# Two blocks of a transformer on one core: the two heads of an attention pair take turns in the value products

## Chip, cores and metric

The kernel runs on one core of a Trainium2 chip. The metric is the device time of one execution in microseconds (us), a median of several runs. TensorE (PE) multiplies matrices and loads weights (PEld), VectorE (DVE), ScalarE (ACT) and GpSimd (POOL) work on elements, SyncE (SP) and GpSimd issue transfers.

## What is computed

1024 tokens of width 1024 go through two blocks. The first has attention with 8 dilated and 8 neighbourhood heads of width 64, an output projection and a mixture of 16 experts; the second has a linear attention, two recurrences and a convolved feed-forward. The change lies in the first block's attention:

```python
# dilated: three windows per head, merged by their softmax denominators
s = einsum('bhrnqd,bhrnkd->bhrnqk', qb, kb) * HEAD_DIM ** -0.5 - slopes * dist
p = exp(where(valid, s, NEG_INF) - mx); o = einsum(p, vb) / den
out = sum(softmax(lses, axis=0)[..., None] * outs)
# neighbourhood: windows of 8 x 16 on a grid of 16 x 64 tokens, learned relative bias
s = where(mask, einsum('bhijqcd,bhijkld->bhijqckl', qb, kg) * HEAD_DIM ** -0.5 + bias, NEG_INF)
o = einsum('bhijqckl,bhijkld->bhijqcd', softmax(s, axis=(-2, -1)), vg)
```

## The kernel before

Products that need precision are split in high and low parts and made of three products each (`mm3`, L260 to L262); these are the projections. Attention goes over eight pairs of heads, four dilated (`attn_dil`), then four neighbourhood ones (`attn_na`). `proj_qk` of pair p+1 stands behind pair p in the program and reads two units of weights: 2 x 2 x 8 x 3 = 96 records on PE, each of 512 columns. In the third neighbourhood pair the last projection and the opening of the output projection come in between its halves (`mid`).

A dilated pair has two halves u, and in each the heads e = 0, 1 one after the other. For a head: eight score blocks j of 128 x 256 (L495, L496) into PSUM; VectorE adds the bias and takes the extremum (L498); ScalarE makes exponentials and their sums (L500). The statistics of two windows are brought to a common row order with two small products (`swap`, L442), merged by small VectorE steps (L506 to L516) and give factors, by which VectorE scales the eight blocks (L520). Then, for jj = 0 to 3, PE transposes four squares of 128 x 128 (L525) into one PSUM tile `tp`, ScalarE copies it to `pt` (L528; for jj = 3 VectorE, L530), and PE multiplies 128 x 64 columns of values with each square (L540) into `y`: head 0 into partitions 0 to 63, head 1 into 64 to 127. Values and weights are in f32, and the trace shows two records for each such product. `finish_pair` copies `y` (L429) and stores it.

A neighbourhood pair has two halves i; for each head and each of four column groups c: two score products of 384 columns (L578), bias and extremum (L582) against `nbias`, which GpSimd makes from the mask (L563), exponentials (L584), reciprocal (L585) and scaling (L586), three transposes (L590), a copy (L592 on ScalarE for even c, L594 on VectorE for odd), three value products (L597).

The framework's scheduler fixes the order on each engine when the program is built, by program order as priority and by its own estimate of what is ready, and it puts the waits. A tag's `bufs` is the number of buffers that its tiles share: the weights of a head (`P`) have two, the transposed ones (`PT`) three, `tp` two in PSUM, `sp` two.

Later in the kernel, the S5 recurrence has products of the same shape as the value products (L1464), from 64 columns of weights, whose outputs go by turns to partitions 0 to 63 and 64 to 127:

```python
for g in range(2):
    r = slice(64 * g, 64 * g + 64)
    nc.tensor.matmul(pz[r, i, pi % 2], E[pi // 4][:, pi % 4, i, r], U[:, 2 * pi + g], start=True, stop=True,
```

Of the kernel before, what the change touches and what calls it, by code (L numbers as in the profile page):

```python
# [12 lines left out]
OP = mybir.AluOpType  # L13
# [5 lines left out]
# Places of the experts by falling load: place 0 has room for 256 tokens, the next NMORE places for 192, the others for 128.  # L19
# JOBS: the order of work.  # L20
# [7 lines left out]
# ---------------------------------------------------------------- host layout  # L28
def _units_f(w, cols):
    """[1024, *] -> one unit [128, 8*128] per block of 128 columns (contraction on partitions)."""  # L30
    return np.stack([np.ascontiguousarray(w[:, c:c + 128]).reshape(8, 128, 128).transpose(1, 0, 2).reshape(128, 1024)
                     for c in cols])


def _units_n(w, n0, n1):
    """[K, *] -> units [128, 2*512] of two contraction tiles by 512 columns."""
    k = w.shape[0] // 256
    return np.ascontiguousarray(w[:, n0:n1]).reshape(k, 2, 128, 512).transpose(0, 2, 1, 3).reshape(k, 128, 1024)
# [24 lines left out]
def _na_mask():  # L63
# [12 lines left out]
    return out.reshape(128, 6, 384)  # L76
# [20 lines left out]
def _route_consts():  # L97
    """upper[t', t] = t' < t, what a logit's lead over another must exceed (the first wins a tie), 0..15"""
# [14 lines left out]
def prep(inp):  # L113
# [31 lines left out]
    # ---- block 2  # L145
# [40 lines left out]
# ---------------------------------------------------------------- device  # L186
class K:
# [34 lines left out]
    def wraw(self, src, eng=None, after=None):  # L222
        """a unit of weights; after: what must be there before the load may take its turn"""
# [17 lines left out]
    def rstd(self, ssq, n, out):  # L241
        """out = 1/sqrt(ssq/n + eps), [128, m]"""
# [4 lines left out]
    def rstd_pow(self, ssq, n, out):  # L247
        """out = (ssq/n + eps) ** -0.5, without the square root's activation table"""
# [15 lines left out]
    def norm_rows(self, x, gb, out, st, sq=None):  # L264
        """out = x / rms(x) * g on rows; st [128, 2]; sq: room for the squares"""
# [5 lines left out]
    def rows_T(self, xn, XH, XL, i, ps):  # L271
        """rows of token tile i to columns, hi and lo"""
# [10 lines left out]
    # ------------------------------------------------ block 1, attention  # L283
    def attention(self, rs):
        """attention heads in pairs, and the output projection"""
        nc, a = self.nc, self.a
        from contextlib import ExitStack
        with ExitStack() as st, ExitStack() as sl, ExitStack() as sr:
# [44 lines left out]
            self.mask = wk.tile([128, 6, 384], F32, name="mask_n")  # L333
# [35 lines left out]
    def tm_proj(self, out, XH, XL, W, j):  # L369
        """rows of token tile j times 512 columns of weights"""  # L370
# [5 lines left out]
    def proj_qk(self, XH, XL, p):  # L376
        """-> of two heads, q's hi over lo (the odd head: lo over hi), and k's hi twice and lo twice"""
# [54 lines left out]
    def swap(self, src, n, to_a):  # L432
        """statistics of class rows (32b+i, r) to block rows (4i+r, b), or back; src [128, n, 4]"""
# [13 lines left out]
        out = wk.tile([128, n, 4], F32, tag="swo", name="swo", bufs=2)  # L447
# [3 lines left out]
    def attn_dil(self, p, q0, k0, q1, k1):  # L451
# [18 lines left out]
        for u in range(2):  # L470
            y = ps.tile([128, 512], F32, tag="y", name="y", bufs=2)
            for e in range(2):
                PP = wk.tile([128, 8, 256], F32, tag="P", name="PP", bufs=2)
                stt = wk.tile([128, 2, 2, 4], F32, tag="stat", name="stat", bufs=3)  # A/B, nm/den, j
                for j in range(8):
                    if j % 2 == 0:
                        sp = ps.tile([128, 2, 256], F32, tag="s", name="sp", bufs=2)
                    if j < 4:
                        r = j
                        lh = Q[e][:, r, 128 * u:128 * u + 128]  # L480
                        rh = [Kk[e][:, s, r, 16:272] for s in range(2)]
                        bs = bias[e][:, 256 * (3 + u):256 * (4 + u)]
                        stj = (1, j)
                    else:
                        b = 4 * u + j - 4
                        lh = (q0, q1)[e][:, 128 * b:128 * b + 128]
                        rh = []
                        for s in range(2):
# [1530 lines left out]
```

## Time and profile before

| | us |
|---|---|
| median of 3 runs (2163.27 to 2168.06) | 2163.78 |
| span of the profiled execution | 2164.2 |
| dilated pairs in it, about | 133 to 388 |
| neighbourhood pairs, about | 388 to 580 |

The profile is of one execution. Busy times are sums over an engine's instructions without counting overlaps twice; records of PE overlap since products are pipelined, so the distance from start to start tells more than the length of one. "Clock" is the share of full speed that TensorE was granted.

### The profile page before, as it was taken

The numbers are of one execution on the slowest core, as the hardware profiler recorded it, in microseconds if no ns is written. First come the engines' busy times: TensorE is split into PE (matmuls) and PEld (weight loads), VectorE is DVE, ScalarE is ACT, GpSimd is POOL, SyncE is SP. The second block draws the span as 40 slices with busy tenths as digits, with TensorE's granted clock in tenths as the row PEclk, the third lists the DMA queues.
The fourth block names the chain that finished last, engine by engine and source line by source line (L and its number), as shares of the span: only waits on it lengthen the run. The fifth ranks groups of instructions, "written<-read, shape, count | busy, mean of one in ns | idle before, by whom it ended". The sixth has DMA issues, their size and how long they took to land.

```text
span 2164.2 us, 27190 instructions
## 1 busy us (share of the span) xinstructions
PE 2032.3 (94%) x9877; PEld 1627.9 (75%) x9877; DVE 1207.6 (56%) x2613; ACT 820.4 (38%) x1502; POOL 397.5 (18%) x508
## 2 busy tenths in 40 slices
PE   8999999998898799968999979999999999999997
PEld 6878887776687577746877667778888888888886
DVE  4146666555667677758277378854443444443445
ACT  4245544444433477745321653431122111122113
POOL 2111111333342111106255143210000000000001
PEclk9999999999999799988999989999999999999999
DMA  6153322423342799957351276461111111111101
GB/s 238 69 125 92 97 77 61 106 75 105 110 129 74 255 309 316 322 191 261 115 105 44 69 257 209 147 243 40 49 49 59 49 46 37 46 58 49 49 10 78
DMA packets 123232, 260.71 MB, mean 120 GB/s; under 512 B 21872, under 2 KB 67216, under 8 KB 122448
## 3 DMA queue, kind: packets, MB, share of 16 engines
q1 hardware_dynamic: 103584, 195.94, 28.1%
q0 software_dynamic: 16800, 61.61, 8.9%
q10 hardware_dynamic: 2704, 1.31, 0.3%
q8 instruction: 81, 1.33, 0.3%
q14 instruction: 63, 0.52, 0.1%
HBM read 196.10 MB, written 53.22 MB: 115 GB/s over the span
## 4 chain that ended last, share of the span: by engine, by line
PE 43%; DVE 5%; POOL 2%; DMA 2%; issue 1%; ACT 1%; SPq 0%; POOLq 0%; DVEq 0%; ACTq 0%
PE pu L260 4%; PE pu L262 4%; PE pu L261 4%; PE pv L262 4%; PE pd L260 4%; PE pv L261 4%; PE pv L260 4%; PE pd L262 4%; PE pd L261 4%; PE pvg L262 1%; PE pvg L260 1%; PE pvg L261 1%; PE pp L260 1%; PE pp L262 1%; PE pp L261 1%
## 5 line engine op out<-in xcount | busy, mean ns | idle before, releaser
L237 ACT CAST whi<-wraw 128x1024 fp32r<-128x1024 f32 x188 | 197.4, 1050 | 608.4 <-PE pd L262 189.9
L238 DVE TENSOR_TENSOR wlo<-wraw,whi 128x1024 fp32r<-128x1024 f32 x162 | 197.9, 1222 | 271.9 <-ACT whi L237 269.0
L260 PE MATMUL pp<-XH,whi 128*128 128x512 f32 x416 | 168.2, 404 | 0.6 <-DVE kk L404 0.5
L261 PE MATMUL pp<-XL,whi 128*128 128x512 f32 x416 | 167.7, 403 | 0.0
L262 PE MATMUL pp<-XH,wlo 128*128 128x512 f32 x416 | 166.7, 401 | 0.0
L1940 DVE TENSOR_TENSOR res<-pd,res 128x512 f32<-128x512 f32 x176 | 118.4, 689 | 85.0 <-PE pd L262 85.0
L260 PE MATMUL pd<-whi,fah 128*128 128x512 f32 x352 | 138.3, 393 | 0.0
L260 PE MATMUL pu<-XH,whi 128*128 128x512 f32 x352 | 137.8, 392 | 0.0
L261 PE MATMUL pu<-XL,whi 128*128 128x512 f32 x352 | 137.6, 391 | 0.0
L262 PE MATMUL pu<-XH,wlo 128*128 128x512 f32 x352 | 137.6, 391 | 0.0
L261 PE MATMUL pd<-wlo,fah 128*128 128x512 f32 x352 | 137.1, 389 | 0.0
L262 PE MATMUL pv<-XH,wlo 128*128 128x512 f32 x352 | 137.0, 389 | 0.0
L260 PE MATMUL pv<-XH,whi 128*128 128x512 f32 x352 | 136.9, 389 | 0.0
L261 PE MATMUL pv<-XL,whi 128*128 128x512 f32 x352 | 136.9, 389 | 0.0
L1954 POOL TENSOR_TENSOR fo<-res,gfin 128x1024 f32<-128x1024 f32 x3 | 8.0, 2691 | 698.1 <-DVE res L1940 698.1
L262 PE MATMUL pd<-whi,fal 128*128 128x512 f32 x352 | 131.8, 390 | 0.0
L260 PEld LDWEIGHTS pp<-XH,whi 128*128 128x128 f32 x416 | 79.0, 190 | 18.4 <-issue 3.1
L262 PEld LDWEIGHTS pp<-XH,wlo 128*128 128x128 f32 x416 | 78.8, 189 | 15.9 <-issue 2.5
L261 PEld LDWEIGHTS pp<-XL,whi 128*128 128x128 f32 x416 | 79.0, 190 | 15.3 <-issue 2.4
L238 POOL TENSOR_TENSOR wlo<-wraw,whi 128x1024 fp32r<-128x1024 f32 x26 | 62.7, 2413 | 144.0 <-ACT whi L237 105.0
L1926 DVE TENSOR_TENSOR ft<-ft,pv 128x1024 f32<-128x1024 f32 x22 | 26.9, 1222 | 103.2 <-PE pv L262 103.2
L500 ACT ACTIVATE PP<-PP,stat 128x256 f32<-128x256 f32 x128 | 64.4, 504 | 48.0 <-DVE stat L498 44.1
(563 smaller groups left out, 4901.8 us busy)
## 6 DMA issues: line engine op xcount, KB each, us to landing
wraw<-in_wgu_dram SPq DMA_DIRECT2D x64, 512.0 KB, 4.7
wraw<-in_wup_dram SPq DMA_DIRECT2D x44, 512.0 KB, 3.3
wraw<-in_wdn_dram SPq DMA_DIRECT2D x32, 512.0 KB, 5.0
wraw<-in_wdown_dram SPq DMA_DIRECT2D x22, 512.0 KB, 3.3
O<-ot SPq DMA_DIRECT2D x17, 512.0 KB, 4.9
wraw<-in_win_f_dram SPq DMA_DIRECT2D x16, 512.0 KB, 4.2
x<-x_d SPq DMA_DIRECT2D x16, 512.0 KB, 4.1
x_d<-x SPq DMA_DIRECT2D x16, 512.0 KB, 3.7
```

The source lines that it names most:

```text
L237: nc.scalar.copy(hi, raw)
L238: (eng or nc.vector).tensor_tensor(lo, raw, hi.bitcast(F32), op=OP.subtract)
L260: nc.tensor.matmul(out, lh, rh, start=start, stop=False, **kw)
L261: nc.tensor.matmul(out, lh, rl, start=False, stop=False, **kw)
L262: nc.tensor.matmul(out, ll, rh, start=False, stop=stop, **kw)
L500: nc.scalar.activation(PP[:, j], PP[:, j], AF.Exp, bias=nm, scale=-1.0, accum_out=stt[:, stj[0], 1, stj[1]:stj[1] + 1])
L1926: V.tensor_tensor(t, t, pv, op=OP.mult)
L1940: V.tensor_tensor(self.res[:, j, cn], pd, self.res[:, j, cn], op=OP.add)
L1954: nc.gpsimd.tensor_tensor(o, x, gb, op=OP.mult)
```

## The change

In both kinds of pair the softmax of both heads now comes first, and then the transposes and value products, in which the heads take turns. In the dilated pairs the softmax of a head moves into `dil_weights`, called for both heads; for each jj both heads' squares are transposed and copied, and then the products go i by i, head 0, head 1. In the neighbourhood pairs the scores and softmax of both heads and all four c come first, then c by c both heads' transposes and copies, and their products t by t, head 0, head 1.

The weights of a head are kept in two tiles of half the size, with five such buffers for both heads; `PT` has four. Room for that comes from a mask in bf16 instead of f32 and from fewer buffers of `swo`, `stat`, `mg`, `nM`, `fac`, `statn` and `r1` (the output projection's row factor). Comments are taken out all over the file.

```diff
-    return out.reshape(128, 6, 384)
+    return out.reshape(128, 6, 384).astype(mybir.dt.np(BF16))
...
-            self.mask = wk.tile([128, 6, 384], F32, name="mask_n")
+            self.mask = wk.tile([128, 6, 384], BF16, name="mask_n")
...
-        out = wk.tile([128, n, 4], F32, tag="swo", name="swo", bufs=2)
+        out = wk.tile([128, n, 4], F32, tag="swo", name="swo", bufs=1)
...
             y = ps.tile([128, 512], F32, tag="y", name="y", bufs=2)
-            for e in range(2):
-                PP = wk.tile([128, 8, 256], F32, tag="P", name="PP", bufs=2)
-                stt = wk.tile([128, 2, 2, 4], F32, tag="stat", name="stat", bufs=3)  # A/B, nm/den, j
-                for j in range(8):
...
-                # merge the two softmaxes
...
-                for j in range(8):
-                    f = fb[:, 0, j:j + 1] if j < 4 else fac[:, 0, j - 4:j - 3]
-                    nc.vector.tensor_scalar(PP[:, j], PP[:, j], f, None, op0=OP.mult)
-                for jj in range(4):
+            both = [self.dil_weights(u, e, (q0, q1)[e], Q[e], Kk[e], bias[e]) for e in range(2)]
+            for jj in range(4):
+                pts = []
+                for e, PP in enumerate(both):
                     tp = ps.tile([128, 4, 128], F32, tag="tr", name="tp", bufs=2)
-                    pt = wk.tile([128, 4, 128], F32, tag="PT", name="PT", bufs=3)
+                    pt = wk.tile([128, 4, 128], F32, tag="PT", name="PT", bufs=4)
                     for i in range(4):
-                        nc.tensor.transpose(tp[:, i], PP[:, 2 * jj + i // 2, 128 * (i % 2):128 * (i % 2) + 128],
-                                            self.ident)
+                        nc.tensor.transpose(tp[:, i], PP[jj // 2][:, 2 * (jj % 2) + i // 2,
+                                                                  128 * (i % 2):128 * (i % 2) + 128], self.ident)
                     if jj != 3:
                         nc.scalar.copy(pt, tp)
                     else:
                         nc.vector.tensor_copy(pt, tp)
-                    for i in range(4):
-                        j, kt = 2 * jj + i // 2, i % 2
+                    pts.append(pt)
+                for i in range(4):
+                    j, kt = 2 * jj + i // 2, i % 2
+                    for e, pt in enumerate(pts):
                         if j < 4:
                             yo = y[64 * e:64 * e + 64].rearrange("p (m r) -> p r m", r=4)[:, j]
                             v = VB[:, kt, j, 64 * e:64 * e + 64]
...
                         nc.tensor.matmul(yo, v, pt[:, i], start=(j == 0 and kt == 0), stop=(j == 7 and kt == 1),
                                          skip_group_check=True)
             self.finish_pair(p, u, y)
+    def dil_weights(self, u, e, q, Qr, Kr, bias):
+        nc, wk, ps = self.nc, self.wk, self.ps
+        PP = [wk.tile([128, 4, 256], F32, tag="P", name="PP", bufs=5) for _ in range(2)]
+        stt = wk.tile([128, 2, 2, 4], F32, tag="stat", name="stat", bufs=2)
+        for j in range(8):
+            if j % 2 == 0:
+                sp = ps.tile([128, 2, 256], F32, tag="s", name="sp", bufs=2)
+            if j < 4:
...
+            so = sp[:, j % 2]
+            nc.tensor.matmul(so, lh, rh[0], start=True, stop=False)
+            nc.tensor.matmul(so, lh, rh[1], start=False, stop=True)
+            nm = stt[:, stj[0], 0, stj[1]:stj[1] + 1]
+            nc.vector.tensor_tensor_reduce(out=PP[j // 4][:, j % 4], in0=so, in1=bs, op0=OP.add, op1=OP.min, scale=1.0,
+                                           scalar=3e38, accum_out=nm)
+            nc.scalar.activation(PP[j // 4][:, j % 4], PP[j // 4][:, j % 4], AF.Exp, bias=nm, scale=-1.0,
+                                 accum_out=stt[:, stj[0], 1, stj[1]:stj[1] + 1])
...
+        bt = self.swap(stt[:, 1], 2, True)
+        m2 = wk.tile([128, 2, 2, 4], F32, tag="mg", name="m2", bufs=2)
+        nM = wk.tile([128, 4], F32, tag="nM", name="nM", bufs=2)
...
+        fac = wk.tile([128, 2, 4], F32, tag="fac", name="fac", bufs=2)
+        nc.vector.tensor_tensor(fac, m2[:, 1], nM[:, None, :].to_broadcast([128, 2, 4]), op=OP.mult)
+        fb = self.swap(fac[:, 1:2], 1, False)
+        for j in range(8):
+            f = fb[:, 0, j:j + 1] if j < 4 else fac[:, 0, j - 4:j - 3]
+            nc.vector.tensor_scalar(PP[j // 4][:, j % 4], PP[j // 4][:, j % 4], f, None, op0=OP.mult)
+        return PP
...
+            PQ = [[], []]
             for e in range(2):
-                PQ = wk.tile([128, 4, 384], F32, tag="P", name="PQ", bufs=2)
                 for c in range(4):
+                    if c % 2 == 0:
+                        PQ[e].append(wk.tile([128, 2, 384], F32, tag="P", name="PQ", bufs=5))
                     sp = ps.tile([128, 384], F32, tag="s", name="sp", bufs=2)
                     lh = (q0, q1)[e][:, 512 * i + 128 * c:512 * i + 128 * c + 128]
                     for s in range(2):
                         nc.tensor.matmul(sp, lh, Kk[e][:, s, 4 * i:4 * i + 12, NA_CS[c]:NA_CS[c] + 32],
                                          start=(s == 0), stop=(s == 1))
-                    PN = PQ[:, c]
-                    stt = wk.tile([128, 2], F32, tag="statn", name="statn", bufs=4)
+                    PN = PQ[e][c // 2][:, c % 2]
+                    stt = wk.tile([128, 2], F32, tag="statn", name="statn", bufs=3)
                     nc.vector.tensor_tensor_reduce(out=PN, in0=sp, in1=nb[e][i][:, (0, 1, 1, 2)[c]], op0=OP.add,
                                                    op1=OP.min, scale=1.0, scalar=3e38, accum_out=stt[:, 0:1])
                     nc.scalar.activation(PN, PN, AF.Exp, bias=stt[:, 0:1], scale=-1.0, accum_out=stt[:, 1:2])
                     nc.vector.reciprocal(stt[:, 1:2], stt[:, 1:2])
                     nc.vector.tensor_scalar(PN, PN, stt[:, 1:2], None, op0=OP.mult)
+            for c in range(4):
+                pts = []
+                for e in range(2):
                     tp = ps.tile([128, 3, 128], F32, tag="tr", name="tp", bufs=2)
-                    pt = wk.tile([128, 4, 128], F32, tag="PT", name="PT", bufs=3)
+                    pt = wk.tile([128, 4, 128], F32, tag="PT", name="PT", bufs=4)
                     for t in range(3):
-                        nc.tensor.transpose(tp[:, t], PN[:, 128 * t:128 * t + 128], self.ident)
+                        nc.tensor.transpose(tp[:, t], PQ[e][c // 2][:, c % 2, 128 * t:128 * t + 128], self.ident)
                     if c % 2 == 0:
                         nc.scalar.copy(pt[:, 0:3], tp)
                     else:
                         nc.vector.tensor_copy(pt[:, 0:3], tp)
-                    yo = y[64 * e:64 * e + 64].rearrange("p (R C) -> p R C", C=64)[:, :, 16 * c:16 * c + 16]
-                    for t in range(3):
-                        nc.tensor.matmul(yo, VN[:, c, i + t, 64 * e:64 * e + 64], pt[:, t],
+                    pts.append(pt)
+                for t in range(3):
+                    for e in range(2):
+                        yo = y[64 * e:64 * e + 64].rearrange("p (R C) -> p R C", C=64)[:, :, 16 * c:16 * c + 16]
+                        nc.tensor.matmul(yo, VN[:, c, i + t, 64 * e:64 * e + 64], pts[e][:, t],
                                          start=(c == 0 and t == 0), stop=(c == 3 and t == 2), skip_group_check=True)
             self.finish_pair(4 + p, i, y)
...
-                r = yp.tile([128, 1], F32, tag="r1", name="r1", bufs=2)
+                r = yp.tile([128, 1], F32, tag="r1", name="r1", bufs=1)
```

## Rows read from the trace of the kernel before

**Rows 1.** The page's part 1: engines, busy us and share.

```profile
PE 2032.3 (94%) x9877; PEld 1627.9 (75%) x9877; DVE 1207.6 (56%) x2613; ACT 820.4 (38%) x1502; POOL 397.5 (18%) x508
```

**Rows 2.** Stretches: us, PE, PEld, DVE, ACT, POOL busy, clock, DMA share, GB/s.

```profile
133.00:388.00 255.00, 250.06 (x1489) 206.11 (x1489) 160.77 (x674) 132.84 (x366) 35.82 (x39) 0.99 0.28 77
388.00:540.00 152.00, 142.61 (x788) 110.44 (x787) 88.30 (x240) 65.27 (x153) 56.15 (x56) 0.97 0.35 96
540.00:580.00 40.00, 35.68 (x216) 26.85 (x216) 29.83 (x85) 16.05 (x43) 12.51 (x16) 0.96 0.09 30
...
519.00:578.00 59.00, 50.57 (x288) 36.98 (x286) 44.40 (x122) 29.21 (x74) 21.10 (x24) 0.91 0.23 79
```

**Rows 3.** Waits of PE, 133 to 580 us: sum, times, longest.

```profile
PE tp L590 <- DVE PQ L586: 3.7, 5, 2.1
PE tp L590 <- DVE statn L585: 3.4, 1, 3.4
PE sp L495 <- DMA kk<-kk: 3.1, 1, 3.1
```

**Rows 4.** Lines of PE, whole trace: busy us, mean ns, idle before.

```profile
L540 PE MATMUL y<-PT,VV 128*64 128x128 f32 x512 | 66.4, 277 | 0.9 <-ACT PT L528 0.2
...
L597 PE MATMUL y<-PT,VV 128*64 128x128 f32 x384 | 54.0, 291 | 2.6 <-ACT PT L592 2.0 <-DVE r L250 0.5
```

**Rows 5.** Time line of PE in a dilated half-pair: start, length, what.

```profile
149.39 1.03 PE L525 MATMUL tp<-ident,PP 128*128 128x128 f32 x8
...
150.67 1.96 PE L540 MATMUL y<-PT,VV 128*64 128x128 f32 x16
152.56 1.09 PE L525 MATMUL tp<-ident,PP 128*128 128x128 f32 x8
...
153.89 1.96 PE L540 MATMUL y<-PT,VV 128*64 128x128 f32 x16
...
165.92 1.09 PE L540 MATMUL y<-PT,VV 128*64 128x128 f32 x8
```

**Rows 6.** Time line of PE, products of the S5 recurrence.

```profile
1126.46 5.01 PE L1464 MATMUL pz<-U,s5E 128*64 128x128 f32 x64 [4.13 <-DMA s5KT<-s5G]
```

**Rows 7.** Stretches within those products, columns as in rows 2.

```profile
1126.40:1129.10 2.70, 2.64 (x26) 2.67 (x28) 2.63 (x3) 0.59 (x1) 0.00 (x0) 0.50 0.36 39
1129.50:1131.30 1.80, 1.80 (x36) 1.68 (x32) 0.60 (x1) 1.18 (x2) 0.00 (x0) 1.00 0.65 66
```

**Rows 8.** Time line of PE in the first neighbourhood half-pair.

```profile
392.30 1.52 PE L597 MATMUL y<-PT,VV 128*64 128x128 f32 x12
...
395.10 1.15 PE L597 MATMUL y<-PT,VV 128*64 128x128 f32 x12
...
401.50 0.87 PE L597 MATMUL y<-PT,VV 128*64 128x128 f32 x6
```

**Rows 9.** Lines of ScalarE, 133 to 387 us.

```profile
L528 ACT COPY PT<-tp 128x512 f32<-128x512 f32 x48 | 27.0, 588 | 38.0 <-PE tp L525 37.9
```

**Rows 10.** A stretch between two neighbourhood pairs, columns as in rows 2.

```profile
417.00:432.00 15.00, 15.00 (x68) 12.31 (x66) 3.44 (x5) 3.40 (x5) 4.10 (x4) 1.00 0.78 177
```

**Rows 11.** Lines of VectorE, 133 to 387 us.

```profile
L498 DVE CUSTOM_DVE_ANT_0 PP<-sp,bias 128x256 f32<-128x256 f32 x128 | 53.4, 422 | 22.7 <-PE sp L496 20.6
L520 DVE TENSOR_SCALAR PP<-PP,fac 128x256 f32<-128x256 f32 x64 | 23.8, 393 | 0.0
```

**Rows 12.** Waits of VectorE, 133 to 580 us, columns as in rows 3.

```profile
DVE PQ L582 <- POOL nbias L563: 2.7, 3, 0.9
DVE statn L585 <- ACT PQ L584: 1.9, 3, 1.2
```

**Rows 13.** The mask's instructions: count, ns min/median/max, first and last start.

```profile
L563 POOL TENSOR_TENSOR nbias<-mask_n,rpbE x48: 985/1013/1463, 342.6 to 558.6; 128x384 f32<-128x384 f32 x48
L334 SPq DMA_DIRECT2D mask_n<-in_mask_n_dram x1: 328/328/328, 99.8 to 99.8; - x1
```

**Rows 14.** A stretch after the stop for the keys, columns as in rows 2.

```profile
134.00:138.00 4.00, 4.00 (x15) 3.52 (x14) 2.85 (x11) 2.28 (x8) 0.00 (x0) 0.50 0.63 229
```

More of the change, by code (lines that the diff above doesn't have):

```diff
@@ L542, in attn_dil @@
             self.finish_pair(p, u, y)
+    def dil_weights(self, u, e, q, Qr, Kr, bias):
[6 more added lines that the diff above has]
+            if j < 4:
+                r = j
+                lh = Qr[:, r, 128 * u:128 * u + 128]
+                rh = [Kr[:, s, r, 16:272] for s in range(2)]
+                bs = bias[:, 256 * (3 + u):256 * (4 + u)]
+                stj = (1, j)
+            else:
+                b = 4 * u + j - 4
+                lh = q[:, 128 * b:128 * b + 128]
+                rh = []
+                for s in range(2):
+                    kw = Kr[:, s, :, 32 * b:32 * b + 64].rearrange("p r (t j) -> p t r j", t=2)
+                    rh.append(kw)
+                v = 0 if b == 0 else 2 if b == 7 else 1
+                bs = bias[:, 256 * v:256 * v + 256]
+                stj = (0, j - 4)
+            so = sp[:, j % 2]
[9 more added lines that the diff above has]
+        nM = wk.tile([128, 4], F32, tag="nM", name="nM", bufs=2)
+        nc.vector.tensor_tensor(nM, stt[:, 0, 0], bt[:, 0], op=OP.min)
+        nc.vector.tensor_tensor(m2[:, 0, 0], nM, stt[:, 0, 0], op=OP.subtract)
+        nc.vector.tensor_tensor(m2[:, 0, 1], nM, bt[:, 0], op=OP.subtract)
+        nc.scalar.activation(m2[:, 1], m2[:, 0], AF.Exp)
+        nc.vector.tensor_tensor(m2[:, 0, 0], m2[:, 1, 0], stt[:, 0, 1], op=OP.mult)
+        nc.vector.tensor_tensor(m2[:, 0, 1], m2[:, 1, 1], bt[:, 1], op=OP.mult)
+        nc.vector.tensor_tensor(nM, m2[:, 0, 0], m2[:, 0, 1], op=OP.add)
+        nc.vector.reciprocal(nM, nM)
+        fac = wk.tile([128, 2, 4], F32, tag="fac", name="fac", bufs=2)
[5 more added lines that the diff above has]
+        return PP
```

40 lines of the change are left out of this document (removed).

## The prediction, made before the result was known

> **What bounds the kernel now.** The page comes first: TensorE (PE) is busy 94% of the span, the other engines 18 to 56% [rows 1]. That is an average, so next come the stretches: in the dilated pairs (133 to 388 us) PE is busy 250.1 of 255 us, in the neighbourhood pairs to 540 us 142.6 of 152, in the last stretch of attention 35.7 of 40, while VectorE reaches 160.8 of 255 and, in that last stretch, 29.8 of 40 [rows 2]. The waits of PE between 133 and 580 us are few: 3.1 us for a copy of the keys, 3.7 and 3.4 us for scaled weights [rows 3]. So PE's own work sets the time of attention, except in the last three half-pairs (519 to 578 us), where PE is busy 50.6 of 59 us at a mean granted clock of 0.91, VectorE 44.4, and no projection of a further pair is left to fill gaps [rows 2]. The profile's span is 2164.2 us, the median of the runs 2163.78; I count from the span.
>
> What PE does there is read by lines: 512 records of the dilated value products (L540), 384 of the neighbourhood ones (L597) [rows 4]. Each product has two records: 4 pairs x 2 halves x 2 heads x 16 products are 256 products. They load 64 columns of weights, so each head uses half the columns of the array.
>
> **The serial pitch.** In the time line a run of 16 records of one head takes 1.96 us and one record alone 0.273 us [rows 4, 5]: (1.96 - 0.27)/15 = 0.113 us from start to start; for a run of eight, (1.09 - 0.27)/7 = 0.117. Leaving a run also costs: the last start of the first run is 150.67 + 1.96 - 0.27 = 152.36 us and the next transpose starts at 152.56, 0.20 us later [rows 5].
>
> **The pitch when two heads alternate.** The kernel already has products of the same shape (L1464, 128 rows, 64 columns, 128 moving) whose outputs alternate between partitions 0 to 63 and 64 to 127. Their 64 records start and end in 5.01 us [rows 6]. The run begins at the lower clock, 0.50 (1.2 GHz), where 26 records fall in 2.70 us, 0.104 us each; at granted clock 1.00 (2.4 GHz) 36 fall in 1.80 us, 0.050, or 0.058 if the five already under way at its start (0.27 us long, one each 0.055) are left out [rows 7]. I take 0.055 at full clock: half the serial pitch, so two records run side by side.
>
> A nearer row stands in the neighbourhood part. Runs of 12 records take 1.52 us when they belong to one head, but 1.15 us in the one run of a half-pair where, in the compiled order, three products of head 0 are followed by three of head 1 [rows 8]. Even head after head, without alternation, 0.37 us of overlap appears.
>
> The Trainium skill speaks against this ("TensorE: Matmul & The Clock Gate", section "Part 3: Packing small matmuls — row/col tiling"): it says that a weight load overlaps running products only where the row group differs. Both heads here use all 128 rows, so by that rule the pitch would stay near 0.11 us and the value products would give back nothing. The trace disagrees: L1464 loads 128 rows for both halves too, and alternates at about 0.055 us.
>
> **The change part by part, value products.** Dilated, per half-pair (u): now two runs of 16 and four of eight. Start to start they take 2 x 1.69 + 4 x 0.82, and six exits 6 x 0.20: 7.86 us. After it, four runs of 16 with heads taking turns: two streams of eight side by side, 0.82 + about 0.05 + exit 0.20 = 1.07 us each, 4.3 us; 3.6 us less. But the order on PE is made from when operands are ready: head 0's copy out of PSUM (0.588 us on ScalarE [rows 9]) precedes head 1's, so head 0's first products may be placed ahead and the turn-taking becomes head after head. Then a run gains only the 0.37 us of rows 8: 1.69 - 0.37 + 0.20 = 1.52, four of them 6.1 us; 1.8 us less. Eight half-pairs: 14 to 29 us.
>
> Neighbourhood, per half-pair (i): now, as in the first, runs of 6, 12, 12, 12, 6: 2 x 0.60 + 2 x 1.25 + 0.88 + 5 x 0.20 = 5.58 us [rows 8]. After, four runs of 12: 0.60 + 0.05 + 0.20 = 0.85 each, 3.4 us, 2.2 less; with head after head 0.88 + 0.20 = 1.08 each, 4.3 us, 1.26 less. Eight of them: 10 to 17 us. Together 24 to 46 us of PE time; I take the middle, 35, since rows 6 and rows 8 are equally near.
>
> **What keeps it from the end.** In the last three half-pairs PE already waits for others, so I count nothing there: 3 x 1.7 = 5 us off, 30 left.
>
> The price is the order: both heads' weights now come before any transposition. Now head 0's transposes and products (149.39 to 155.8 us, 6.4 us [rows 5]) run while head 1's softmax is on VectorE and ScalarE. Afterwards that cover is gone, and the next cover is the projection of the following pair, 96 records at 15.0/68 = 0.22 us [rows 10]: 21 us a pair. It suffices if VectorE keeps up. Per dilated half-pair VectorE is busy 160.8/8 = 20.1 us and ScalarE 132.8/8 = 16.6 us [rows 2], against a period of 31.9 us that would become about 29. VectorE's main terms there are 0.42 us for each score block and 0.39 us for each scaling [rows 11]. And in the neighbourhood part filler is left over: from 417 to 432 us PE runs projections alone, VectorE busy 3.4 of 15 us [rows 10]; these can move under the longer softmax. Bounds: nothing where filler covers, 6.4 us a half-pair where it does not. Near the covered end, I charge a tenth of the gain, 3 us. What is queued behind PE's new wait is the next jj's transposes and the next half-pair's scores, and behind those VectorE. The fifth weights buffer lets the next half's first four blocks go during the products.
>
> **Everything else.** The counts of transposes, copies, exponentials and scalings are unchanged. The wider PT (3 to 4 buffers) holds two steps of both heads. The single swo, and two of stat, m2, nM and fac, are read on VectorE, which runs in order, so reuse waits for what has already run; stat is also read on ScalarE, long before the next half-pair needs it. Three statn buffers instead of four touch a chain in which VectorE waits 1.9 us in all for ScalarE [rows 12], so at most about that is added. r1 with one buffer: the next tile's factor is wanted a whole tile later than the last reader of the old one; nothing. The mask in bf16 halves a load issued at 99.85 us, with no reader until 342.6 us [rows 13]: no gain on the path. The subtraction that reads it takes 1.0 us, 48 times, on GpSimd [rows 13], and VectorE waited only 2.7 us for it [rows 12], so a gain is at most 2.7 us; a slower one is hidden while GpSimd itself waits. I take nothing for all of these, and 3 us either way in the range.
>
> Sum: 35 - 5 - 3 = 27 us: 2164.2 - 27 = **2137 us**.
>
> **The rivals.** (a) No overlap: the column halves do not run side by side for these operands, or the order on PE comes out with transposes or projections between the heads' runs. Against it rows 6 to 8; for it the copies that become ready one after the other. Left would be the fewer exits, 6 to 4 and 5 to 4 per half-pair, 24 x 0.2 = 5 us, less 3 to 5 us of lost cover: 2162 to 2164. By the page's rule above the same time would result. Chance 0.08.
>
> (b) VectorE takes over: PE gets its 35 us, but the softmax of both heads in one piece becomes the chain, and PE waits for scaled weights. For it: PE's 3.7 and 3.4 us waits [rows 3] are of this kind, and VectorE is at 75% in the last 59 us. If half the gain is lost so, 2164 - 13 = 2151. Chance 0.17.
>
> (c) Slower: the lost cover is not replaced. At the transposes after both softmaxes PE stands idle, and the granted clock falls to 0.50, as it did after the 3.1 us stop for the keys (0.50 from 134 to 138 us [rows 14]). This decides from the point where idle time per half-pair exceeds 35/16 = 2.2 us. At 4 us in each of 16: 64 - 35 = 29 us, 2193. For it: no filler from 519 to 578 us; against it: 21 us of filler in each earlier pair. Chance 0.10.
>
> **How the numbers follow.** The forecast has chance 0.65, its own range 2116 (46 us and 2 off) to 2148. About 0.2% (4.3 us) is what a measurement here can tell from no change, so faster means below 2159.5. The forecast and (b) are faster (0.82), (a) mostly the same (0.08), (c) slower (0.10). The range reaches over (b): 2117 to 2158, leaving (a), (c) and a little at the low end out.
>
> **What would show it.** In the trace after: runs of 16 value products near 1.1 us (forecast) or 1.6 (head after head), not 2; in neighbourhood runs of 12 near 0.9 to 1.15; the busy time of the two value-product lines down from 66.4 and 54.0 us [rows 4] towards 40 and 35; PE's waits for scaled weights below 10 us in sum; the end of attention 20 to 30 us earlier and everything after it unchanged. I am wrong if those runs stay at 1.9 us, if the waits on scaled weights exceed 20 us, or if the granted clock is 0.50 for long between 140 and 520 us.

## The result, and the profile after

The median fell from 2163.88 us (2163.27 to 2168.06, 4 runs) to 2142.64 us (2139.68 to 2146.43, 4 runs): ratio 0.9896, 95% interval 0.9878 to 0.9914. The forecast was 2137 us in a range of 2117 to 2158, so direction and size came out. The profiled execution has a span of 2140.0 us, against 2164.2.

The engines, as in [rows 1]: TensorE (PE) is busy 23.6 us less and its weight loads (PEld) 32.5 us less; the others change by at most 3.2.

```profile
PE 2008.7 (94%) x9877; PEld 1595.4 (75%) x9877; DVE 1206.5 (56%) x2613; ACT 821.6 (38%) x1502; POOL 394.3 (18%) x508
```

The two value-product lines, L540 and L597 of [rows 4], are now L497 and L615 (lines of PE from 133 to 560 us; the columns are busy us, mean ns, idle time before):

```profile
L497 PE MATMUL y<-PT,VV 128*64 128x128 f32 x512 | 49.7, 286 | 0.7 <-ACT PT L482 0.7
...
L615 PE MATMUL y<-PT,VV 128*64 128x128 f32 x384 | 42.2, 290 | 0.9 <-ACT PT L607 0.9
```

Busy time went from 66.4 to 49.7 us and from 54.0 to 42.2. How the runs look is in the time line of PE, in a dilated half-pair (start, length, what), where [rows 5] had runs of 16 in 1.96 us:

```profile
160.37 1.09 PE L497 MATMUL y<-PT,VV 128*64 128x128 f32 x14
161.39 0.66 PE L479 MATMUL tp<-ident,PP 128*128 128x128 f32 x4
161.97 0.43 PE L497 MATMUL y<-PT,VV 128*64 128x128 f32 x2
162.34 0.66 PE L479 MATMUL tp<-ident,PP 128*128 128x128 f32 x4
162.92 1.09 PE L497 MATMUL y<-PT,VV 128*64 128x128 f32 x14
163.94 0.66 PE L479 MATMUL tp<-ident,PP 128*128 128x128 f32 x4
```

Two things are to be seen. Fourteen records take 1.09 us, as long as eight of one head took before [rows 5]: the heads do run side by side, (1.09 - 0.27)/13 = 0.063 us from start to start on the mean. Read record by record, all 32 such runs are six pairs and then two single records; in the first one above the two records of a pair start 0.007 us apart, and from the second pair on the pairs follow every 0.109 us. And a step is not one run of 16 but 2 + 14. Head 0's copy is ready first, so (experiment 7 bears this out) the compiled order puts one product of head 0 (two records) ahead, then four transposes of the next step, then the other seven products of the step. That leaves head 1 with all its eight records in the run of 14, so the lone product shortens nothing; it takes 162.34 - 161.97 = 0.37 us of its own, most of it the exit. In the neighbourhood pairs it is 2 + 10 instead of 12:

```profile
426.48 0.87 PE L615 MATMUL y<-PT,VV 128*64 128x128 f32 x10
427.28 0.55 PE L605 MATMUL tp<-ident,PQ 128*128 128x128 f32 x3
427.76 0.43 PE L615 MATMUL y<-PT,VV 128*64 128x128 f32 x2
428.12 0.55 PE L605 MATMUL tp<-ident,PQ 128*128 128x128 f32 x3
```

Below, the **value time** of a kernel is what these runs take of PE: from each run's first start to the start of PE's next other instruction, summed over the whole time line. What a run costs ahead of its first start is not in it. Before it was 113.5 us (63.0 + 50.5, in 49 and 50 runs); now it is 83.0 (45.2 + 37.8, in 64 and 63 runs). So 30.5 us were freed.

PE's waits from 128 to 560 us (sum, times, longest), to be held against [rows 3]:

```profile
PE swp L442 <- DVE swx L439: 5.6, 5, 2.3
PE sp L590 <- DVE statn L594: 4.6, 7, 1.7
PE tp L479 <- DVE PP L551: 3.5, 2, 1.9
PE tp L605 <- DVE PQ L598: 1.2, 3, 0.6
...
PE sp L526 <- DMA kk<-kk: 0.5, 1, 0.5
```

In before (128 to 580 us) the two of these that lie in the dilated pairs were:

```profile
PE tp L525 <- DVE PP L520: 2.1, 2, 1.7
...
PE swp L442 <- DVE swx L439: 0.9, 1, 0.9
```

The waits for scaled weights (L479, L605) are small; the wait at the swapped statistics (L442) has grown by 4.7 us. The wait for the keys (3.1 us in [rows 3]) is almost gone in this execution; the same kernel, run again, had it at 2.5 us, so it is no part of the change.

Where the stretches of attention end is read off the starts of VectorE's copies of `y` (L429): after the last dilated half-pair (the 8th copy), the fifth neighbourhood one (13th) and the last (16th). In the time line of VectorE after:

```profile
369.44 0.69 DVE L429 COPY yo<-y 128x512 f32<-128x512 f32 x1 [1.51 <-PE y L497]
...
481.23 0.69 DVE L429 COPY yo<-y 128x512 f32<-128x512 f32 x1
...
549.99 0.68 DVE L429 COPY yo<-y 128x512 f32<-128x512 f32 x1
```

In before, with the first score product:

```profile
133.20 0.57 PE L495 MATMUL sp<-kk,qq 128*128 128x256 f32 x1 [3.11 <-DMA kk<-kk]
...
383.76 0.69 DVE L429 COPY yo<-y 128x512 f32<-128x512 f32 x1 [2.40 <-PE y L540]
...
502.05 0.69 DVE L429 COPY yo<-y 128x512 f32<-128x512 f32 x1 [1.18 <-PE y L597]
...
578.91 0.69 DVE L429 COPY yo<-y 128x512 f32<-128x512 f32 x1 [0.90 <-PE y L597]
```

The first score product after starts at 130.58 us. The same marks of every kernel give this table of stretches (us; each from one profiled execution):

| kernel | dilated | first five neighbourhood | last three | attention in all | rest of the span |
|---|---|---|---|---|---|
| before | 250.6 | 118.3 | 76.9 | 445.7 | 1585.3 |
| before, second profile | 250.8 | 118.1 | 76.5 | 445.4 | 1589.8 |
| after | 238.9 | 111.8 | 68.8 | 419.4 | 1590.0 |
| after, second profile | 241.6 | 111.8 | 68.7 | 422.1 | 1586.6 |

The dilated pairs gave 9 to 12 us, the neighbourhood pairs 14.6, and, against the prediction, 8 us of these lie in the last three half-pairs. The rest of the span scatters by 4.5 us for one and the same kernel.

### The profile page after: what moved, and what is told of

Same layout as the page of the kernel before. It is cut to its first block, busy times and chain, and to the rows that moved or that the text cites. A ratio compares the mean times of both kernels' runs of the same rounds, so it can differ in the third digit from the quotient of the medians.

```text
span 2140.0 us, 27167 instructions
## 1 busy us (share of the span) xinstructions
PE 2008.7 (94%) x9877; PEld 1595.4 (75%) x9877; DVE 1206.5 (56%) x2613; ACT 821.6 (38%) x1502; POOL 394.3 (18%) x508
## 4 chain that ended last, share of the span: by engine, by line
PE 44%; DVE 5%; POOL 2%; DMA 2%; issue 2%; ACT 1%; SPq 0%; POOLq 0%; DVEq 0%; ACTq 0%
PE pu L260 4%; PE pu L261 4%; PE pu L262 4%; PE pd L260 4%; PE pv L262 4%; PE pv L261 4%; PE pv L260 4%; PE pd L261 4%; PE pd L262 4%; PE pvg L260 1%; PE pvg L262 1%; PE pvg L261 1%; PE pp L260 1%; PE pp L262 1%; PE pp L261 1%
## 5 line engine op out<-in xcount | busy, mean ns | idle before, releaser
L260 PEld LDWEIGHTS pd<-whi,fah 128*128 128x128 f32 x352 | 66.1, 188 | 17.7 <-ACT fah L1947 4.4
```

Source lines behind the costliest of these rows:

```text
L260: nc.tensor.matmul(out, lh, rh, start=start, stop=False, **kw)
```

## The experiments

Each kernel was timed beside runs of before on the same chip; what is given is the ratio to those. All edits are to the kernel after, unless said otherwise.

**1. The order alone, without turns.** Both softmaxes first, but then all transposes and products of head 0, and then those of head 1.

```diff
-            for jj in range(4):
-                pts = []
-                for e, PP in enumerate(both):
+            for e, PP in enumerate(both):
+                for jj in range(4):
...
-            for c in range(4):
-                pts = []
-                for e in range(2):
+            for e in range(2):
+                for c in range(4):
```

> The changed kernel, but the value products of head 0 all come before those of head 1, each with its own transposes between; both softmaxes still come first, buffers and mask as in the changed kernel. Theory A (the gain is two heads' products side by side in the two column halves): the 36 us of TensorE time come back, the waits that the new order made (about 8 us on swapped statistics and scaled weights) stay, 2164 to 2172 us. Theory B (the gain is in buffers, mask and the number of runs): 2143 to 2150 us.

Measured: 2171.88 us, ratio 1.0026 (1.0011 to 1.0042), so slightly slower than before. Value time is 114.7 us: runs are back at 1.96 us for 16 records.

```profile
163.22 1.96 PE L493 MATMUL y<-PT,VV 128*64 128x128 f32 x16 [2.03 <-ACT PT L481]
```

The whole gain comes from the turns, and the order by itself costs something. PE's longest waits (128 to 580 us) are:

```profile
PE swp L442 <- DVE swx L439: 6.8, 6, 2.3
PE sp L586 <- DVE statn L590: 4.7, 8, 1.4
PE y L493 <- ACT PT L481: 3.3, 2, 2.0
```

Most of the first is not the order's: experiment 3 has the old order with the buffers of after, and there it is 5.8 us. What the order without turns adds is the wait of value products for their copies (L493; 0.2 us in before). The dilated stretch is 262.6 us, 12.0 longer than before's, of which value time is 3.8; PE's idle time in it, summed from the trace behind the first score product, is 13.2 us, against 4.7 in before and 6.7 in experiment 3. Its first five neighbourhood half-pairs take 115.5 us and its last three 70.8, 8.9 us less in sum, of which value time is 2.6. The new order costs in the dilated part and gives in the neighbourhood part.

**2. Head after head within a step.** The products of head 0's square, then head 1's, side by side in the order but without alternation.

```diff
-                for i in range(4):
-                    j, kt = 2 * jj + i // 2, i % 2
-                    for e, pt in enumerate(pts):
+                for e, pt in enumerate(pts):
+                    for i in range(4):
+                        j, kt = 2 * jj + i // 2, i % 2
...
-                for t in range(3):
-                    for e in range(2):
+                for e in range(2):
+                    for t in range(3):
```

> The changed kernel, but within a step the products of head 0 all stand before those of head 1, with nothing between them. If neighbouring runs of the two heads overlap by 0.37 us as in the kernel before, a run of 16 with its exit costs 1.52 us against 1.38 now (short run, exit, long run, exit): about 5 to 8 us slower than the changed kernel, 2148 to 2151 us. If only strict turns overlap: 1.89 us a run, 2165 to 2172 us. If the order does not matter as long as both heads stand together: 1.07 us a run, 2130 to 2138 us.

Measured: 2158.57 us, ratio 0.9973 (0.9960 to 0.9985); slower than expected by about 8 us. The overlap where one head follows the other is there, as in [rows 8]: the run takes 1.58 us instead of 1.96, 0.38 less. Read record by record, 23 of the 28 runs of 16 are four single records, four pairs and four single ones: the second half's records begin to start beside the fifth of the first.

```profile
158.92 1.58 PE L496 MATMUL y<-PT,VV 128*64 128x128 f32 x16
```

But in the neighbourhood part only 18 runs of 12 came about (24 stayed single runs of six, 8 are shorter), and value time is 99.3 us: 14.2 freed. About half of what the turns free comes without them.

**3 and 4. The rest of the change alone.** The order of before with the buffers and the mask of after; and before with nothing but the mask in bf16.

```diff
-            both = [self.dil_weights(u, e, (q0, q1)[e], Q[e], Kk[e], bias[e]) for e in range(2)]
-            for jj in range(4):
-                pts = []
-                for e, PP in enumerate(both):
+            for e in range(2):
+                PP = self.dil_weights(u, e, (q0, q1)[e], Q[e], Kk[e], bias[e])
+                for jj in range(4):
```

> The order of the kernel before (softmax, transposes and products of head 0, then of head 1) with all buffers and the mask of the changed kernel. Theory A: 2160 to 2165 us. Theory B: 2143 to 2150 us.

The second, against before:

```diff
-            self.mask = wk.tile([128, 6, 384], F32, name="mask_n")
+            self.mask = wk.tile([128, 6, 384], BF16, name="mask_n")
```

> The kernel before with nothing but the mask in bf16. The first score product began 2.6 us earlier in the changed kernel, since the copy of the keys landed earlier. If the smaller mask load did that: first score product at 130.6 us and 2161 us in all. If it is a matter of one execution or of the other tiles' places: 2163 to 2165 us.

Measured: 2163.59 us, ratio 0.9994 (0.9976 to 1.0011), and 2162.76 us, ratio 0.9986 (0.9971 to 1.0001). Buffers and mask have no effect that shows; a gain of a few us by the mask is not excluded by the second interval, but the first kernel has the same mask. The second kernel's first score product starts at 131.35 us, between the two cases of its expectation, and before itself has 133.20 and 132.54 us in two profiles, so this decides nothing.

Within experiment 3 something did move. In its dilated pairs PE's waits for scaled weights are gone, and the one at the swapped statistics is as long as in after:

```profile
PE swp L442 <- DVE swx L439: 5.8, 5, 2.7
```

It comes with the buffers, then, and not with the new order; which part of the new buffers makes it was not tested.

**5 and 6. One part at a time.** Turns in the dilated pairs alone (neighbourhood loop in the old order), and in the neighbourhood pairs alone (dilated loop as in experiment 3).

```diff
-            for c in range(4):
-                pts = []
-                for e in range(2):
...
-                for t in range(3):
-                    for e in range(2):
+                    for t in range(3):
```

> The changed kernel with the neighbourhood pairs back in the order of the kernel before (softmax, transposes, products head by head). In the profile of the changed kernel the dilated pairs took 11.8 us less from the first score product to their last copy of y, the neighbourhood ones 14.5 us. If the two add: 12 us less than before, 2152 us (2149 to 2155). If the neighbourhood pairs' gain was in truth filler moved over from the dilated ones: 2143 to 2147 us or above 2158 us.

> The changed kernel with the dilated pairs back in the order of the kernel before. If the two parts add: 14 us less than before, 2150 us (2147 to 2153). If not: as for the other half.

Measured: 2154.90 us, ratio 0.9946 (0.9931 to 0.9961), and 2157.79 us, ratio 0.9966 (0.9953 to 0.9978): 11.7 and 7.4 us less. Together 19.1, against 20.8 to 22.5 for both at once, so the parts add up within their intervals. The second was expected larger (2147 to 2153 us). In its profile the neighbourhood stretches are 14.4 us shorter, as in after, but the rest of the span is 1591.9 us, 2.1 to 6.6 longer than in the two profiles of before.

**7. Both heads in one copy.** Each PSUM tile takes squares of both heads, so that their products become ready together. In the neighbourhood pairs each copy takes three squares, in the order t by t, head 0, head 1.

```diff
-                for e, PP in enumerate(both):
+                for h in range(2):
...
-                    for i in range(4):
-                        nc.tensor.transpose(tp[:, i], PP[jj // 2][:, 2 * (jj % 2) + i // 2, ...
+                    for k in range(2):
+                        for e, PP in enumerate(both):
+                            nc.tensor.transpose(tp[:, 2 * k + e], PP[jj // 2][:, 2 * (jj % 2) + h, ...
...
-                    for e, pt in enumerate(pts):
+                    for e in range(2):
...
-                        nc.tensor.matmul(yo, v, pt[:, i], ...
+                        nc.tensor.matmul(yo, v, pts[i // 2][:, 2 * (i % 2) + e], ...
```

> The changed kernel, but each copy out of PSUM carries transposed squares of both heads (two of each in a dilated pair, three in all in a neighbourhood pair), so that both heads' products become ready at the same time. In the changed kernel a dilated step runs as 2 records, exit, 14 records, exit (1.38 us); now 16 in one run (about 1.02 us): 12 us of TensorE time less; the neighbourhood runs stay as many. Theory A with TensorE still the bound: 2132 to 2138 us. If VectorE and ScalarE now set the time: 2141 to 2146 us.

Measured: 2132.82 us, ratio 0.9847 (0.9834 to 0.9860), as expected. In the dilated pairs runs of 16 now exist (26, all of them eight pairs, and 12 runs of eight):

```profile
161.49 1.14 PE L497 MATMUL y<-PT,VV 128*64 128x128 f32 x16 [0.22 <-ACT PT L483]
```

(1.14 - 0.27)/15 = 0.058 us from start to start, the pitch of [rows 7]. A run of 16 costs 0.05 us more than the run of 14 above; the lone products of after bought nothing. With the exit, 16 records now take 1.08 us of PE, where 2 + 14 took 1.02 + 0.37 = 1.39.

**8. Squares of both heads in fours, in the neighbourhood pairs too.** Experiment 7, and there three copies of four squares (two heads by two) in place of four of three for each two column groups.

```diff
-            for c in range(4):
-                pts = []
-                for e in range(2):
-                    tp = ps.tile([128, 3, 128], F32, tag="tr", name="tp", bufs=2)
+            for cp in range(2):
+                for m in range(3):
+                    tp = ps.tile([128, 4, 128], F32, tag="tr", name="tp", bufs=2)
...
-                    for t in range(3):
-                        nc.tensor.transpose(tp[:, t], PQ[e][c // 2][:, c % 2, 128 * t:128 * t + 128], self.ident)
+                    for k in range(4):
+                        c, t = divmod(6 * cp + 2 * m + k // 2, 3)
+                        nc.tensor.transpose(tp[:, k], PQ[k % 2][cp][:, c % 2, 128 * t:128 * t + 128], self.ident)
```

> As the kernel whose copies carry both heads, and in the neighbourhood pairs three copies of four squares (two of each head) for two column groups in place of four copies of three squares; the runs there become 8 or 16 records in turns. Another 10 us of TensorE time less, and two copies less per half-pair. TensorE still the bound: 2122 to 2131 us. If the softmax chain sets the time: 2136 to 2144 us.

Measured: 2120.72 us, ratio 0.9791 (0.9778 to 0.9804): faster than both kernels and 1.3 us below the range that was expected. Value time is 62.1 us, 7.7 less than in experiment 7, while the timed gain is 12.1 us larger; the two copies less in each half-pair are a part of this edit as well. Lines of PE, 125 to 545 us, and two of its neighbourhood runs in the time line:

```profile
L497 PE MATMUL y<-PT,VV 128*64 128x128 f32 x512 | 37.0, 283 | 3.7 <-ACT PT L483 2.5 <-DVE PT L485 1.0
L614 PE MATMUL y<-PT,VV 128*64 128x128 f32 x384 | 29.9, 286 | 1.5 <-DVE PT L609 1.2 <-ACT PT L607 0.2
```

```profile
375.64 1.13 PE L614 MATMUL y<-PT,VV 128*64 128x128 f32 x16
378.03 1.15 PE L614 MATMUL y<-PT,VV 128*64 128x128 f32 x16
```

**9. Turns in the same half.** The heads take turns as in after, but head 1's products go onto partitions 0 to 63 too, in both windows and in the neighbourhood pairs. So `y` holds the sum of both heads: the kernel leaves out keeping them apart. `finish_pair` copies only these partitions, and GpSimd fills the others of `yo` with zeros.

```diff
-                            yo = y[64 * e:64 * e + 64].rearrange("p (m r) -> p r m", r=4)[:, j]
+                            yo = y[0:64].rearrange("p (m r) -> p r m", r=4)[:, j]
```

> The changed kernel, but head 1's products go to partitions 0 to 63 as well, on top of head 0's, so both heads use the same half of the columns; partitions 64 to 127 of the copy are filled with zeros. It leaves out that the two heads' outputs are kept apart: y holds their sum. The products, weights, copies and turns are the same in number. Theory A (the halves run side by side): the pitch goes back to 0.11 us, a run of 14 records to about 1.47 us from first to last start, 22 to 25 us of TensorE time back in the dilated and 12 to 16 in the neighbourhood pairs, 2170 to 2182 us in all. If alternating weights alone, in any columns, make the pitch: run of 14 stays at 0.82 us, 2143 us.

Measured: 2172.29 us, ratio 1.0036 (1.0021 to 1.0052). Order, copies out of PSUM and count of the products are those of after, and so are the dilated runs (32 of 14 and 32 of two); the columns that the products occupy differ, and the run of 14 takes 1.74 us instead of 1.09:

```profile
164.15 0.43 PE L498 MATMUL y<-PT,VV 128*64 128x128 f32 x2
164.51 0.66 PE L480 MATMUL tp<-ident,PP 128*128 128x128 f32 x4
165.10 1.74 PE L498 MATMUL y<-PT,VV 128*64 128x128 f32 x14
```

(1.74 - 0.27)/13 = 0.113 us, the serial pitch of [rows 4, 5]. Read record by record there is no pair left, in any run. Both heads now write the same places of PSUM by turns, but that does not make the pitch: in before one head's products of the first window go on to other places with every second product, and in the run at 150.67 us [rows 5] the records start 0.109 us apart there too. That the outputs lie in different column halves is what makes the records run side by side.

**10, 11 and 12. Repeats.** After and the kernel of experiment 8 beside each other, and before again for a second profile.

> The changed kernel once more, on the chip of this call, to set the last call's versions beside it: ratio to the kernel before 0.990 (0.988 to 0.992).

> The version with copies of both heads and quads once more, on the same chip as the changed kernel: 0.979 of the kernel before, and 20 to 24 us below the changed kernel.

> The kernel before once more, for a second profile of it. Everything behind the last copy of attention's output took 1585.3 us in the first profile of before and 1587 to 1592 us in those of eight other kernels, one of which (only buffers and mask changed) has the old order. Theory A: this stretch differs from execution to execution, and this profile shows 1587 us or more. Theory B: the changed order gives some 4 us back after attention; then this profile shows 1584 to 1586. The first score product is expected between 131 and 134 us, the time within 2160 to 2168 us.

Measured: 2144.12 us (0.9904, 0.9887 to 0.9921) and 2118.49 us (0.9791, 0.9773 to 0.9808), 25.6 us apart, a little more than the 20 to 24 expected; before again 2166.70 us, ratio 1.0002 (0.9983 to 1.0020), with the last copy of `y` in its profile at

```profile
577.88 0.69 DVE L429 COPY yo<-y 128x512 f32<-128x512 f32 x1 [0.89 <-PE y L597]
```

in a span of 2167.7 us. So the rest of its span is 1589.8 us, as long as after's.

All in one table: value time, the change of attention's length against 445.7 us, and the timed change (ratio less one, times 2165 us). Attention is that of the one profiled execution, the timed change is from the medians:

| kernel | value time, us | its change | attention | timed |
|---|---|---|---|---|
| 1, order alone | 114.7 | +1.2 | +3.2 | +5.6 |
| 9, same half | 118.9 | +5.4 | +4.2 | +7.8 |
| 4, mask alone | 113.3 | -0.2 | -4.8 | -3.0 |
| 3, buffers and mask | 112.5 | -1.0 | -0.7 | -1.3 |
| 6, neighbourhood alone | 101.1 | -12.4 | -13.6 | -7.4 |
| 2, head after head | 99.3 | -14.2 | -12.8 | -5.8 |
| 5, dilated alone | 94.2 | -19.3 | -11.8 | -11.7 |
| after | 83.0 | -30.5 | -26.3, -23.6 | -22.5, -20.8 |
| 7, both in one copy | 69.8 | -43.7 | -38.0 | -33.1 |
| 8, fours | 62.1 | -51.4 | -49.1 | -45.2 |

In experiment 4 attention is 4.8 us shorter at the same value time, so a difference of that size in this column need not be the products'.

## Why the prediction held, step by step

**The bound.** PE's own work sets the time of attention: over the rows of the table, from +5 to -51 us of value time, the timed change follows with 2 to 11 us of loss where the order is new, and with none where it is old (experiments 3 and 4).

**The pitch.** Right. It was taken from another line of the same kernel, the products of L1464, and the value products show it: 0.058 us where a full run forms (experiment 7), against 0.113 in one half (experiment 9). The Trainium skill's rule that was weighed ("TensorE: Matmul & The Clock Gate", section "Part 3: Packing small matmuls — row/col tiling") is that a weight load overlaps running products only where the row group differs. The runs do not bear out what was drawn from it for this shape: all loads in experiment 9 and in after use all 128 rows, the two differ in the column half of head 1, and the pitch is 0.113 against 0.063 us.

**The size of the value products.** Right in sum, 30.5 us against the middle of 35 in 24 to 46, but by errors that partly cancel, so that it came so near is luck in part. The prediction left them 8 x 4.3 + 8 x 3.4 = 61.6 us with full turns, 83.2 with head after head, and took the middle, 72. What was left is 83.0; that this is near the 83.2 is chance, since the mechanism is another. It had seen that head 0's copy is ready first and drew from it that the heads would follow each other; in fact one product goes ahead, the other seven keep their turns, and each step pays a second exit: 64 + 63 runs rather than 32 + 32. On the other side the base was undersized: the first neighbourhood half-pair, with its three runs of 12, is not typical (36 runs of six and 14 of 12 over the eight), so the base was 113.5 us, not 8 x 7.86 + 8 x 5.58 = 107.5. Experiment 8, in which the runs are not split, leaves 62.1 us: the estimate for full turns was within 1 us.

**Nothing in the last three half-pairs (-5 us).** Wrong: they became 8 us shorter. Experiment 1 has 6.1 us of that without turns, experiment 3 with the old order 0.6 (76.3 us), so it is mostly the order that shortens them: PE's idle time there is 8.4 us in before and 5.4 in experiment 1. From experiment 1 to after the turns free another 4.6 us of value time there (19.1 to 14.5), and the stretch gets only 2.0 us shorter. So the prediction was not far off on the turns; the gain by the order is what it did not have. Why the order gains there was not tested; it is consistent with [rows 3], where PE waited for each head's scaled weights just before their transposes.

**The order's price (-3 us).** Too small for the dilated part. There 63.0 - 45.2 = 17.8 us of value time were freed and the stretch is 9.0 to 11.7 shorter. PE's idle time in it rose from 4.7 to 10.8 us. The predicted waits for scaled weights are there (3.5 us at L479, 2.1 in before), but the larger one is 5.6 us at the products of the swapped statistics (L442), and experiment 3 has this one without the new order. In the neighbourhood pairs PE's idle time fell, from 12.9 to 7.6 us, so that over attention as a whole it hardly changed: 17.6 us before, 18.5 after.

So the waits are not what keeps attention from becoming 30.5 us shorter. The transposes are, and the prediction has no term for them. Four of them take 0.35 us of PE when a projection follows, and 0.58 when value products do (161.39 to 161.97 in the time line of after above). The first case in before, in the half-pair of [rows 5]:

```profile
162.72 0.60 PE L525 MATMUL tp<-ident,PP 128*128 128x128 f32 x4
163.07 0.49 PE L260 MATMUL pp<-XH,whi 128*128 128x512 f32 x1
```

From the last transpose's start to the first value product 0.20 us pass, to a projection 0.03 (medians over attention). In before 21 runs of value products stand right behind transposes, in after 76; as an estimate, 55 more at 0.17 us make 9.4. Summed as the value time is, without idle time, the transposes of attention took 50.9 us in before and 60.2 in after; in experiment 7, where the runs are not split, 51.0. The prediction priced leaving a run, 0.20 us [rows 5], and not entering one. Of these 9.3 us the projections gave back 5.6 (171.6 to 166.0 us).

Both deductions together were 8 us; the timed loss, 30.5 - 20.8 to 22.5, is 8 to 10, of which 4 to 7 lie in attention and the rest where executions scatter. The total was right, its places were not: that is luck.

**Everything else at nothing.** Held for the time, by experiment 3; for the mask alone, within 0.3%. It did not hold for the waits: with the smaller buffers PE's idle time in the dilated pairs is 6.7 us instead of 4.7, and 5.8 us of PE's waits come at the swapped statistics.

**The rivals.** (a) No overlap: experiment 9 is this case, and it takes 2172 us. (b) VectorE takes over half: a part of the gain, a quarter to a third (8 to 10 of 30.5 us), does go, and the two waits of the dilated pairs are 6 us longer; but over attention PE waits no longer than before, so this is not where the part went. (c) Slower: its mechanism occurs in small. After the 1.62 us stop that ends at 154.55 us the granted clock falls to 0.50 (1.2 GHz) from 156.20 to 159.61 us (stretch of PE, columns as in [rows 2]), and a run of 14 in it takes 1.87 us:

```profile
154.55 0.63 PE L479 MATMUL tp<-ident,PP 128*128 128x128 f32 x4 [1.62 <-DVE PP L551]
...
156.06 1.87 PE L497 MATMUL y<-PT,VV 128*64 128x128 f32 x14
```

```profile
156.00:160.00 4.00, 4.00 (x27) 2.96 (x25) 2.26 (x6) 3.22 (x7) 1.06 (x2) 0.57 0.64 146
214.00:218.00 4.00, 3.43 (x14) 2.95 (x14) 3.69 (x15) 0.58 (x1) 0.00 (x0) 0.57 0.42 131
```

There are two such spells among the dilated pairs, 6.8 us in all, not one in each half-pair, so it stays far from 2.2 us of idle time per half-pair. Before has 6.0 us at this level there, at the stop for the keys [rows 14]; the second profile of after has 13.7, and its dilated stretch is 2.7 us longer.

**The end of attention and what follows.** 20 to 30 us earlier was right (28.9 in the first profile, of which 2.6 us are the earlier start). The rest looked 4.7 us longer; the second profile of before shows 1589.8 us against 1590.0, so this is the difference between executions. What causes it stays open, and with it why experiments 2 and 6 gained 6 to 7 us less in time than their attention shortened. For experiment 2, 3.4 us of this are its profiled execution, which took 2155.16 us against a median of 2158.57; for experiment 6 it was the median itself.

## What to carry to other kernels

Products that fill only half of the array's columns are worth placing in turns with products of the other half; look for a line in the same trace that already alternates, and take its pitch. Then see to it that the operands of both become ready together, best in one copy: a scheduler that places by readiness splits the run otherwise, and each split is paid at both ends, 0.20 us on leaving a run and 0.20 on entering one from transposes. A price that is read off one end shows only half of it; sum the neighbours' time too. And before a new wait is put down to a new order, look for it in a kernel that has the rest of the change and the old order: here it was there as well.

## What the runs showed of the hardware

- Records of the two column halves run side by side without strict alternation: eight of one half followed by eight of the other take 0.38 us less than sixteen of one (experiment 2), with four pairs in the middle.
- In turns, a run is set by its fuller half: 14 records (six and eight) take as long as eight of one half, 1.09 us, as six pairs and two single records.
- Alternation within one half brings nothing (experiment 9): 0.113 us from start to start.
- Between products on 64 columns and transposes on 128 there are 0.20 us from start to start, in either direction, against 0.109 within a run of value products in one half and 0.03 from a transpose to a projection (before and after).
